# The low part of every fourth half tile of weights made by an accumulating DMA instead of by VectorE

## The chip, the core and the metric

The kernel runs on one core of a Trainium2 chip. The metric is device time in microseconds (us) for one execution; lower is better. A core has five engines with a queue each: TensorE (PE, matrix products; its weight loads are a row of their own, PEld), VectorE (DVE), ScalarE (ACT), GpSimd (POOL) and SyncE (SP, which here only issues DMAs). Engines work through their own queues in order and wait for each other by semaphores. Sixteen DMA engines move data; DMAs can be issued from SP's, ACT's and POOL's queues.

## What is computed

One layer of a decoder trunk on 256 tokens of width 2048, in float32:

```
h    = rmsnorm(x, pre_norm_g)
proj = h @ w_in                     # 2048 x 18448: keys, queries, values, gates of all heads
y_a  = (rmsnorm(gla_chunked(...)) * silu(a_g)) @ w_branch_a     # gated linear attention, 4 heads
y_b  = (rmsnorm(diff_attention(...)) * silu(b_g)) @ w_branch_b  # differential attention, 16 heads
merged = sigmoid(m_a) * y_a + sigmoid(m_b) * y_b
x    = x + rmsnorm(merged @ w_out, post_norm_g)
```

Nearly all the arithmetic is in the products with `w_in`, `w_branch_a`, `w_branch_b` and `w_out`, 2048 rows each, and each weight is used once.

## The kernel before

**Products in three parts.** TensorE multiplies in a rounded format (float32r). To keep float32's accuracy each operand is split into a high part (rounded) and a low part (the rest), and a product is hi x hi + hi x lo + lo x hi: three matmuls for one (`product`, L286). The activations are split once and stay in SBUF. The weights are split as they stream in.

**The weight stream** (L106 to L170). The host lays all weights out in the order of use. `chunk_plan` (L28) gives that order: values and low-rank gate, keys and queries of the linear attention, its output gates, two groups of differential heads, the 16 merge gates and branch-a products in turn, two more groups of heads, the merge gates of b, the branch-b products, the output projection. A tile of raw weights holds 2048 elements on each of 128 partitions (1 MB; less for the values) and is loaded by one DMA from SP's queue (L136) into one of three `raw` buffers. It is used in two halves of 1024. `emit_half` (L120) does one half: ScalarE copies it to float32r (`hi`, L155), and VectorE subtracts that from the raw half (`lo`, L156). The pool `wpool` has three buffers of each of `raw`, `hi` and `lo`. There are 392 halves; `take` (L163) hands out the next one and emits ahead as far as `AHEAD` = 4 halves. The last eight halves (`o3`) are kept for use twice and go to buffers of the pool `big`.

**The consumers.** `token_major` (L291) and `channel_major` (L306) take halves and issue 24 matmuls of 256 columns for a half, or 12 of up to 512. In a channel-major half the order of the three is (hi, xh), (hi, xl), (lo, xh).

**Head work between the products.** Forget gates, scores, softmax, head norms and transposes are written as generators in a list, `tasks`; `pump` (L280) lets them take a step behind each product or two, so their instructions stand between those of the stream on every engine. GpSimd does a few adds and the power -1/2 of the norms (`rsqrt`, L239). A scheduler then fixes each engine's order; the program's order of emission is what it goes by.

**Buffers.** `big` has 32 buffers of 4 KB a partition, one tag, for everything long-lived (split activations, gates, values, merged output). `small` holds short-lived tiles.

Of the kernel before, what the change touches and what calls it, by code (L numbers as in the profile page):

```python
# [6 lines left out]
F32 = mybir.dt.float32  # L7
F32R = mybir.dt.float32r
BF16 = mybir.dt.bfloat16
U8 = mybir.dt.uint8  # L10
AF = mybir.ActivationFunctionType
ALU = mybir.AluOpType
AX = mybir.AxisListType

P = 128
D = 2048
# [4 lines left out]
LEVELS = (1, 2, 4, 8, 16, 32, 64)  # L21
VG = (416, 416, 416, 416, 400)
RANK = 16
AHEAD = 4
WARM = 8


def chunk_plan():  # L28
    """Order of the weight chunks: (key, kind, source, columns, elements of a partition)."""
    plan = []  # L30
    at = 0
    for g, n in enumerate(VG):
        lr = RANK if g == 0 else 0
        plan.append((f"v{g}", "tok", "w_in", ([(6144, RANK)] if lr else []) + [(2048 + at, n - lr if lr else n)]))
        at += n - lr
    for hf in range(2):
        for name, base in (("k", 1024), ("q", 0)):
            for c in range(4):
                plan.append((f"{name}{hf}{c}", "chan", "w_in", [(base + 512 * hf + P * c, P)]))
    for g in range(4):  # L40
        plan.append((f"ag{g}", "tok", "w_in", [(4096 + 512 * g, 512)]))
    o = 6144 + RANK

    def heads(g):
        plan.append((f"dv{g}", "tok", "w_in", [(o + 4096 + 512 * g, 512)]))
        plan.append((f"bg{g}", "tok", "w_in", [(o + 6144 + 512 * g, 512)]))
        for pair in range(2):
            for n, name in enumerate(("dq", "dk")):
                for c in (2 * pair, 2 * pair + 1):
                    plan.append((f"{name}{g}{c}", "chan", "w_in", [(o + 2048 * n + 512 * g + P * c, P)]))  # L50

    def gate(br, f):
        plan.append((f"m{br}{f}", "chan", "w_in", [(o + 8192 + 2048 * br + P * f, P)]))

    def branch(br, f):
        plan.append((f"y{br}{f}", "chan", ("w_branch_a", "w_branch_b")[br], [(P * f, P)]))

    heads(0)
    heads(1)
    for f in range(KT):  # L60
        gate(0, f)
        branch(0, f)
    heads(2)
    heads(3)
    for f in range(KT):
        gate(1, f)
    for f in range(KT):
        branch(1, f)
    for g in range(4):
        plan.append((f"o{g}", "tok", "w_out", [(512 * g, 512)]))  # L70
    return plan
# [3 lines left out]
def hybrid_kernel(ctx: ExitStack, tc, xt, xn, preg, postg, w, w2, gkb, glag, lamv, diffg, ident_d, causal_d, lmask_d, out):  # L75
    nc = tc.nc
    pe, act, dve, pool, sp = nc.tensor, nc.scalar, nc.vector, nc.gpsimd, nc.sync

    const = ctx.enter_context(tc.tile_pool(name="const", bufs=1))
    wpool = ctx.enter_context(tc.tile_pool(name="wpool", bufs=3))  # L80
    big = ctx.enter_context(tc.tile_pool(name="big", bufs=32))
    small = ctx.enter_context(tc.tile_pool(name="small", bufs=2))
    psum = ctx.enter_context(tc.tile_pool(name="psum", bufs=4, space=bass.MemoryType.PSUM))

# [2 lines left out]
    def u(shape, name, dtype=F32):  # L87
        count[0] += 1
        return big.tile(shape, dtype, tag="u", name=f"{name}_{count[0]}")
# [13 lines left out]
    def f32(ap):  # L103
        return ap.bitcast(F32)

# [1 line left out]
    plan = chunk_plan()  # L107
    halves = []
    off = 0
    for key, kind, _, cols in plan:  # L110
        n = sum(c for _, c in cols)
# [5 lines left out]
    emitted = [0]  # L117
    raws = {}

    def emit_half():  # L120
        j = emitted[0]
        emitted[0] += 1
        key, at, size, h = halves[j]
        if h == 0:
            raws[at] = wpool.tile([P, 2048], F32, tag="raw", name=f"raw_{at}")
        raw = raws[at]
        src = w[at : at + P * size].rearrange("(p n) -> p n", p=P)
        n = size // 2
        fine = 2 if j == 0 else 1
        if h == 0:  # L130
            if j == 0:
                load_x(0, 1)
            elif j < 8:
                load_x(2 * j, 2)
            for a, b in ((0, n // 2), (n // 2, n), (n, size)) if j == 0 else ((0, n), (n, size)) if j < 8 else ((0, size),):
                i = sp.dma_start(raw[:, a:b], src[:, a:b])  # L136
                if j < 8:
                    tc.keep_in_program_order(i)
                if b == n // 2:
                    load_x(1, 1)  # L140
            if j < 8:
                load_x(2 * j + 2, 2)
        if j < 8:
            prep_x(2 * j)
            if j:
                prep_x(2 * j + 1)
        if key == "o3" and j + 1 < len(halves):
            hi_t, lo_t = u([P, 1024], "keep", F32R), u([P, 1024], "keep", F32R)
        else:
            hi_t = wpool.tile([P, 1024], F32R, tag="hi", name=f"hi_{j}")  # L150
            lo_t = wpool.tile([P, 1024], F32R, tag="lo", name=f"lo_{j}")
        for i in range(fine):
            a, b = n * i // fine, n * (i + 1) // fine
            r = raw[:, n * h + a : n * h + b]
            act.activation(hi_t[:, a:b], r, AF.Copy)  # L155
            dve.tensor_tensor(out=lo_t[:, a:b], in0=r, in1=f32(hi_t[:, a:b]), op=ALU.subtract)  # L156
            if j == 0 and i == 0:
                prep_x(1)
        ready[j] = (key, hi_t, lo_t)
# [3 lines left out]
    def take(key):  # L163
        j = used[0]
        used[0] += 1
        while emitted[0] < min(j + 1 + AHEAD, len(halves)):
            emit_half()
        name, hi, lo = ready.pop(j)
        assert name == key, (name, key)
        return hi, lo  # L170

# [1 line left out]
    xh = [u([P, 4, S], "xh", F32R) for _ in range(4)]  # L173
    xl = [u([P, 4, S], "xl", F32R) for _ in range(4)]
    preg_s = const.tile([P, KT], F32, name="preg_s")
# [4 lines left out]
    def load_x(kt, n):  # L180
        tc.keep_in_program_order(sp.dma_start(xraw[kt // 4][:, kt % 4 : kt % 4 + n, :], xt[:, kt : kt + n, :]))

    def prep_x(kt):
        i, j = kt // 4, kt % 4
        src = xraw[i][:, j, :]
        g = preg_s[:, kt : kt + 1]
        hi = xh[i][:, j, :]
        copied = act.activation(hi, src, AF.Copy, scale=g)  # L188
        if kt == 1:
            tc.keep_in_program_order(copied)  # L190
        dve.scalar_tensor_tensor(out=xl[i][:, j, :], in0=src, scalar=g, in1=f32(hi), op0=ALU.mult, op1=ALU.subtract)  # L191
# [76 lines left out]
        dve.tensor_scalar(out=neg_lam, in0=dots[:, 1:2], scalar1=dots[:, 0:1], scalar2=-LAM_INIT, op0=ALU.subtract, op1=ALU.add)  # L268
        dve.tensor_scalar(out=diffg_s, in0=diffg_s, scalar1=1.0 - LAM_INIT, scalar2=None, op0=ALU.mult)

# [1 line left out]
    def x_ops(kt):  # L272
        return xh[kt // 4][:, kt % 4, :], xl[kt // 4][:, kt % 4, :]

# [48 lines left out]
        act.activation(hi, bank, AF.Copy, scale=gain)  # L323
        dve.scalar_tensor_tensor(out=lo, in0=bank, scalar=gain, in1=f32(hi), op0=ALU.mult, op1=ALU.subtract)

# [1 line left out]
    vh = [u([P, 2, 512], "vh", F32R) for _ in range(4)]  # L327
    vl = [u([P, 2, 512], "vl", F32R) for _ in range(4)]
    lr = u([P, 2, P], "lr")
# [86 lines left out]
            lam()  # L416
            tasks.append(forget_gate())

# [1 line left out]
    att = [None, None]  # L420

    def view(t, off, *dims):
# [95 lines left out]
                pump(1)  # L518
        tasks.append(gla_scores(hf, ts["q"], ts["k"]))

# [1 line left out]
    oah = [u([P, 2, 2, S], "oah", F32R) for _ in range(4)]  # L522
    oal = [u([P, 2, 2, S], "oal", F32R) for _ in range(4)]

# [36 lines left out]
    gates = []  # L561
# [6 lines left out]
        if g % 2:  # L568
            tasks.append(gla_out(g // 2, gates[g - 1 :]))

# [1 line left out]
    obh, obl = [], []  # L572

    def diff_split(g, pair, tq, tk, q2, kh, kl):
# [103 lines left out]
            tasks.insert(0, diff_split(g, pair, *ts, *parts))  # L678
            tasks.append(diff_pair(g, pair, *parts, vv, uu))

# [1 line left out]
    def a_ops(kt):  # L682
        h, j = kt // 4, kt % 4
        i = 2 * (h // 2) + j // 2
        return oah[i][:, j % 2, h % 2, :], oal[i][:, j % 2, h % 2, :]
# [34 lines left out]
    for f in range(KT):  # L720
        o = channel_major(f"y1{f}", b_ops)
        i, j = f // 4, f % 4
# [4 lines left out]
        act.activation(hi, t, AF.Copy, scale=0.5)  # L727
        dve.scalar_tensor_tensor(out=ml[i][:, j, :], in0=t, scalar=0.5, in1=f32(hi), op0=ALU.mult, op1=ALU.subtract)

# [1 line left out]
    pg = [u([P, 1024], "pg") for _ in range(2)]  # L731
    for i in range(2):
        sp.dma_start(pg[i], postg[1024 * i : 1024 * i + 1024].partition_broadcast(P))
# [21 lines left out]
    def subtotal(b, parts):  # L755
        r = sm([P, 1], "or", bufs=2)
        dve.tensor_reduce(out=r, in_=ssq[:, b, :parts], op=ALU.add, axis=AX.X)
        dve.tensor_scalar(out=r, in0=r, scalar1=1.0 / D, scalar2=EPS, op0=ALU.mult, op1=ALU.add)
        return r
# [30 lines left out]
    for c in range(2):  # L790
        bank = ps("mm")
        for kt in range(KT):
            lo = 512 * (kt % 2) + 256 * c
# [3 lines left out]
        if c == 0:  # L797
            square(1, bank[:, :256], 256, 3)
            gain(1, bank[:, :256], 1536, 256)
            r = subtotal(1, 4)  # L800
# [61 lines left out]
```

## Time and profile before

| | us |
|---|---|
| median of two runs (1175.28 and 1175.64) | 1175.46 |
| profiled execution: span from first to last instruction | 1173.6 |
| TensorE matmul busy | 1160.6 |
| TensorE weight loads busy | 1088.4 |
| VectorE busy | 716.9 |
| of it the subtractions that make `lo`, 386 on L156 | 470.5 |
| ScalarE busy | 581.6 |
| of it the copies that make `hi`, 386 on L155 | 401.0 |
| GpSimd busy | 53.6 |

The profiled execution is one more execution than the two timed ones; the page gives its span, and no other time of it. The span is 1.86 us under the median of the timed runs. In the profile's rows a group reads: line, engine, operation, output<-inputs, sizes, count, then busy us and mean ns of one, then the idle time in front of it and what ended that. A row of the waits reads: who waited, on which line, for what; us in total, times, longest. A row of the table by stretches has the stretch and its length, then busy us and count of PE, PEld, DVE, ACT, POOL, then TensorE's granted clock, the DMA engines' busy share and GB/s. A row of DMA issues ends with the size of each and the median us from issue to landing. Matmuls are pipelined and their ends modelled, and a few matmul records can be missing.

### The profile page before, as it was taken

The numbers are of one execution on the slowest core, as the hardware profiler recorded it, in microseconds if no ns is written. First come the engines' busy times: TensorE is split into PE (matmuls) and PEld (weight loads), VectorE is DVE, ScalarE is ACT, GpSimd is POOL, SyncE is SP. The second block draws the span as 40 slices with busy tenths as digits, with TensorE's granted clock in tenths as the row PEclk, the third lists the DMA queues.
The fourth block names the chain that finished last, engine by engine and source line by source line (L and its number), as shares of the span: only waits on it lengthen the run. The fifth ranks groups of instructions, "written<-read, shape, count | busy, mean of one in ns | idle before, by whom it ended". The sixth has DMA issues, their size and how long they took to land.

```text
span 1173.6 us, 19130 instructions
## 1 busy us (share of the span) xinstructions
PE 1160.6 (99%) x7970; PEld 1088.4 (93%) x7970; DVE 716.9 (61%) x1054; ACT 581.6 (50%) x878; POOL 53.6 (5%) x53
## 2 busy tenths in 40 slices
PE   8999999999999999999999999999999999999997
PEld 6999999888889889999999998998999999999886
DVE  7556577657857766665554454565666655666454
ACT  7466343545645655545444334465555544444451
POOL 4010031001000000000000000000000000000000
PEclk9999999999999999999999999999999999999999
DMA  7755544545444444554455555544444445557561
GB/s 268 222 199 210 189 173 172 181 178 190 155 170 167 144 170 154 180 181 149 175 179 181 180 180 187 194 158 180 170 156 178 144 180 180 180 184 290 207 215 72
DMA packets 33799, 211.88 MB, mean 181 GB/s; under 512 B 4192, under 2 KB 5232, under 8 KB 11184
## 3 DMA queue, kind: packets, MB, share of 16 engines
q1 hardware_dynamic: 33104, 209.61, 50.8%
q8 instruction: 62, 1.02, 0.4%
q10 hardware_dynamic: 576, 1.05, 0.2%
q14 instruction: 25, 0.20, 0.1%
q0 software_dynamic: 32, 0.01, 0.0%
HBM read 208.55 MB, written 2.10 MB: 179 GB/s over the span
## 4 chain that ended last, share of the span: by engine, by line
PE 96%; issue 1%; ACT 1%; DVE 1%; DMA 0%; SPq 0%; DVEq 0%; POOLq 0%; POOL 0%; ACTq 0%
PE mm L288 91%; PE bg L484 1%; PE bg L601 1%; PE bg L604 1%; PE bg L288 1%; DMA xraw<-in_xt_dram 0%; PE bg L625 0%; PE bg L635 0%; PE bg L634 0%; PE bg L633 0%; PE bg L552 0%; PE bg L651 0%; ACT xh L188 0%; DVE xl L191 0%; DVE yg L773 0%
## 5 line engine op out<-in xcount | busy, mean ns | idle before, releaser
L156 DVE TENSOR_TENSOR lo<-raw,hi 128x1024 fp32r<-128x1024 f32 (+3 forms) x386 | 470.5, 1220 | 324.1 <-ACT hi L155 321.1
L155 ACT ACTIVATE hi<-raw 128x1024 fp32r<-128x1024 f32 (+3 forms) x386 | 401.0, 1040 | 496.9 <-PE mm L288 478.2
L288 PE MATMUL mm<-xh,hi 128*128 128x256 f32 x1280 | 365.4, 285 | 0.0
L288 PE MATMUL mm<-xh,lo 128*128 128x256 f32 x1280 | 362.2, 283 | 0.0
L288 PE MATMUL mm<-xl,hi 128*128 128x256 f32 x1280 | 362.1, 283 | 0.0
L288 PEld LDWEIGHTS mm<-xh,hi 128*128 128x128 f32 x1280 | 245.5, 192 | 1.5
L288 PEld LDWEIGHTS mm<-xl,hi 128*128 128x128 f32 x1280 | 245.5, 192 | 0.1
L288 PEld LDWEIGHTS mm<-xh,lo 128*128 128x128 f32 x1280 | 245.4, 192 | 0.0
L288 PE MATMUL mm<-hi,xh 128*128 128x512 f32 (+2 forms) x544 | 207.8, 383 | 1.2 <-ACT xh L188 0.9
L288 PE MATMUL mm<-lo,xh 128*128 128x512 f32 (+2 forms) x544 | 205.6, 378 | 2.4 <-DVE lo L156 2.4
L288 PE MATMUL mm<-hi,xl 128*128 128x512 f32 (+2 forms) x544 | 205.6, 378 | 0.8 <-DVE xl L191 0.7
L288 PEld LDWEIGHTS mm<-lo,xh 128*128 128x128 f32 x544 | 102.2, 188 | 18.4 <-DVE lo L156 3.7
L288 PEld LDWEIGHTS mm<-hi,xh 128*128 128x128 f32 x544 | 101.8, 188 | 17.7 <-ACT xh L188 1.3
L288 PEld LDWEIGHTS mm<-hi,xl 128*128 128x128 f32 x544 | 102.1, 188 | 17.1 <-DVE xl L191 1.7
L288 PE MATMUL mm<-oah,hi 128*128 128x256 f32 x256 | 72.8, 284 | 0.0
L288 PE MATMUL mm<-oah,lo 128*128 128x256 f32 x256 | 72.5, 283 | 0.0
L288 PE MATMUL mm<-obh,hi 128*128 128x256 f32 x256 | 72.4, 283 | 0.0
L288 PE MATMUL mm<-obl,hi 128*128 128x256 f32 x256 | 72.4, 283 | 0.0
L288 PE MATMUL mm<-obh,lo 128*128 128x256 f32 x256 | 72.4, 283 | 0.0
L288 PE MATMUL mm<-oal,hi 128*128 128x256 f32 x256 | 72.4, 283 | 0.0
L288 PEld LDWEIGHTS mm<-oah,hi 128*128 128x128 f32 x256 | 49.2, 192 | 0.0
L288 PEld LDWEIGHTS mm<-obh,hi 128*128 128x128 f32 x256 | 49.2, 192 | 0.0
(177 smaller groups left out, 1144.7 us busy)
## 6 DMA issues: line engine op xcount, KB each, us to landing
raw<-in_w_dram SPq DMA_DIRECT2D x176, 1024.0 KB, 4.8
raw<-in_w_dram SPq DMA_DIRECT2D x12, 832.0 KB, 5.6
raw<-in_w_dram SPq DMA_DIRECT2D x4, 800.0 KB, 4.4
raw<-in_w_dram SPq DMA_DIRECT2D x7, 416.0 KB, 6.9
xres<-in_xn_dram SPq DMA_DIRECT2D x4, 512.0 KB, 8.5
xraw<-in_xt_dram SPq DMA_DIRECT2D x7, 256.0 KB, 7.0
lmask<-in_lmask_dram SPq DMA_DIRECT2D x2, 512.0 KB, 8.1
pg<-in_postg_dram SPq DMA_DIRECT2D x2, 512.0 KB, 6.8
```

Source lines behind the costliest of these rows:

```text
L155: act.activation(hi_t[:, a:b], r, AF.Copy)
L156: dve.tensor_tensor(out=lo_t[:, a:b], in0=r, in1=f32(hi_t[:, a:b]), op=ALU.subtract)
L288: i = pe.matmul(out, lhs, rhs, start=first and n == 0, stop=last and n == len(pairs) - 1)
L484: pe.matmul(o, xk[:, P * c : P * c + P], xq.rearrange("p (b c t) -> p b c t", b=2, c=4)[:, :, c, :], start=i == 0, stop=i == 1)
L601: pe.matmul(banks[m][:, lo:up], q2[:, m, i2, t], kh[:, m, i2, :n], start=True, stop=False)
L604: pe.matmul(banks[m][:, lo:up], q2[r, m, i2, t], kl[r, i2, :n], start=False, stop=True)
```

## The change

For every fourth half from half 19 on (`queued`: j % 4 = 3, j at least 16, not in `o3`; 92 halves, always the second half of its raw tile) the low part is no longer made by VectorE. One emission earlier, ScalarE writes the negated, rounded half to a new tile `sum` (three buffers), and GpSimd issues a DMA that adds the raw half to it, SBUF to SBUF. The result, raw minus rounded, is used where `lo` was. `hi` is still made as before. Beside this, `raw` gets a fourth buffer, `AHEAD` becomes 5, `big` has 30 buffers in place of 32, and the scratch for the descriptors of DMAs issued by GpSimd is set to 4096. The other lines of the diff are comments.

```diff
-AHEAD = 4
+AHEAD = 5
...
-    big = ctx.enter_context(tc.tile_pool(name="big", bufs=32))
+    big = ctx.enter_context(tc.tile_pool(name="big", bufs=30))
...
+    sums = {}
+
+    def queued(j):
+        return j % 4 == 3 and 16 <= j < len(halves) and halves[j][0] != "o3"
+
     def emit_half():
...
-            raws[at] = wpool.tile([P, 2048], F32, tag="raw", name=f"raw_{at}")
+            raws[at] = wpool.tile([P, 2048], F32, tag="raw", name=f"raw_{at}", bufs=4)
...
         else:
+            if queued(j + 1):
+                sums[j + 1] = wpool.tile([P, 1024], F32R, tag="sum", name=f"sum_{j + 1}")
+                r = raw[:, n : 2 * n]
+                act.activation(sums[j + 1][:, :n], r, AF.Copy, scale=-1.0)
+                pool.dma_start(sums[j + 1][:, :n], r, accum_op=ALU.add)
             hi_t = wpool.tile([P, 1024], F32R, tag="hi", name=f"hi_{j}")
-            lo_t = wpool.tile([P, 1024], F32R, tag="lo", name=f"lo_{j}")
+            lo_t = sums.pop(j) if queued(j) else wpool.tile([P, 1024], F32R, tag="lo", name=f"lo_{j}")
...
             act.activation(hi_t[:, a:b], r, AF.Copy)
-            dve.tensor_tensor(out=lo_t[:, a:b], in0=r, in1=f32(hi_t[:, a:b]), op=ALU.subtract)
+            if not queued(j):
+                dve.tensor_tensor(out=lo_t[:, a:b], in0=r, in1=f32(hi_t[:, a:b]), op=ALU.subtract)
...
-    nc = bacc.Bacc("TRN2", target_bir_lowering=False, num_devices=1)
+    nc = bacc.Bacc("TRN2", target_bir_lowering=False, num_devices=1, dynamic_dma_scratch_size=4096)
```

## The prediction

> **What bounds the kernel now.** First the head of the page: how much of the span TensorE is busy, and at which clock. Then the two lists of what TensorE's matmul row and its weight-load row waited for, since only such waits can be won. Then a table by stretches, to see where in the span TensorE is idle.
>
> ```profile
> span 1173.6 us, 19130 instructions
> PE 1160.6 (99%) x7970; PEld 1088.4 (93%) x7970; DVE 716.9 (61%) x1054; ACT 581.6 (50%) x878; POOL 53.6 (5%) x53
> PEclk9999999999999999999999999999999999999999
> ...
> PE mm L288 <- DVE lo L156: 2.4, 2, 1.5
> ...
> PEld mm L288 <- DVE lo L156: 3.7, 4, 1.9
> ...
> 0.00:10.00 10.00, 7.87 (x33) 6.30 (x34) 4.11 (x9) 6.36 (x12) 2.17 (x8) 1.00 0.78 224
> ...
> 600.00:800.00 200.00, 200.00 (x1442) 189.35 (x1441) 108.37 (x141) 91.28 (x120) 1.75 (x2) 1.00 0.52 181
> ...
> 1150.00:1174.00 24.00, 15.96 (x116) 15.02 (x114) 7.38 (x15) 1.64 (x6) 1.10 (x2) 0.89 0.24 88
> ```
>
> TensorE is the bound: busy for 99% of the span, all 200 us of the middle stretch, at full clock (1.00). VectorE is at 61% and ScalarE at 50%. What TensorE ever waits for the low parts that VectorE makes is 2.4 us on the matmul row and 3.7 us on the weight-load row, six times in all. Were both lists taken away whole and added, that would be 6.1 us, 0.5% of the span. A measurement of this kernel can tell about 2% from no change; that is 23.5 us of the 1175.46. So relief for VectorE can't win that, and the question is only whether the new work makes TensorE wait.
>
> **How the pipeline breathes.** Three rows of ScalarE's timeline in the merge-gate and branch stretch, then the groups of the two instructions that split a half tile, and what the first waits for:
>
> ```profile
> 621.75 1.06 ACT L155 ACTIVATE hi<-raw 128x1024 fp32r<-128x1024 f32 x1 [1.57 <-PE mm L288]
> 624.62 1.06 ACT L155 ACTIVATE hi<-raw 128x1024 fp32r<-128x1024 f32 x1 [1.81 <-PE mm L288]
> ...
> 633.27 1.06 ACT L155 ACTIVATE hi<-raw 128x1024 fp32r<-128x1024 f32 x1 [1.58 <-PE mm L288]
> ...
> L156 DVE TENSOR_TENSOR lo<-raw,hi 128x1024 fp32r<-128x1024 f32 x345 | 427.4, 1239 | 298.3 <-ACT hi L155 295.6
> ...
> L155 ACT ACTIVATE hi<-raw 128x1024 fp32r<-128x1024 f32 x345 | 365.2, 1059 | 472.2 <-PE mm L288 456.6 <-issue 9.7 <-ACT prob L614 5.5
> ...
> ACT hi L155 <- PE mm L288: 478.2, 296, 2.7
> ```
>
> Four halves pass in 633.27 - 621.75 = 11.52 us, 2.88 us each. There are three buffers of hi, so the hi of half k starts when TensorE has done with half k-3: ScalarE waits 478.2 us in 296 waits for just that. So hi of half k starts two halves before TensorE starts half k, and TensorE has it in time by 2 x 2.88 - 1.06 = 4.7 us.
>
> **The change, part by part.** There are 392 halves; every fourth from half 19 to half 383 is done in the new way, 92 of them. I call such a half m.
>
> *VectorE loses 92 subtractions:* 92 x 1.239 = 114 us of its 716.9. Gain: nothing, since TensorE's six waits for lo are in the first 16 halves or so (the first stretch above has TensorE at 7.87 of 10 us, the middle none idle), and half 19 is the first that changes. I take 0; at most it is 6.1.
>
> *ScalarE gains 92 negations of the same shape as hi:* 92 x 1.059 = 97 us, 581.6 to 679, or 58%. That lies in its 472 us of waiting. What matters is where they stand in its queue. In the built order of the changed program 53 stand right ahead of the hi of half m-5, 33 ahead of that of m-6, four ahead of m-4, and two, for halves 27 and 31, one or two places ahead of their own. Each waits for its raw tile to land, and everything behind it on ScalarE waits too, the next hi first of all.
>
> So: when does raw land? The fourth raw buffer means that the tile with half m goes where the tile of half m-8 was, freed by ScalarE's hi of half m-8 (its VectorE reader is gone, its accumulating DMA was issued eight halves earlier). From the end of that hi to TensorE's start on m-6 there is the time from hi of m-8 to hi of m-4 (that hi starts as TensorE starts on m-6), less the hi itself: 11.52 - 1.06 = 10.46 us. In it must lie the load, the negation (1.06), hi (1.06) and, for the lo of m-6, 1.24 of VectorE, of which TensorE needs the result two matmuls later than hi, so about 1.0; some 0.2 for hand-overs. That leaves 7.1 us for the load from issue to landing where the negation stands ahead of m-6, and 7.1 + 2.88 = 10.0 ahead of m-5.
>
> ```profile
> q1 hardware_dynamic: 33104, 209.61, 50.8%
> ...
> raw<-in_w_dram SPq DMA_DIRECT2D x176, 1024.0 KB, 4.8
> ...
> DMA to landing us min/median/max: 2.6/4.8/8.9
> ...
> xres<-in_xn_dram SPq DMA_DIRECT2D x4, 512.0 KB, 8.5
> ...
> preg_s<-in_preg_dram POOLq DMA_DIRECT2D x1, 8.0 KB, 2.7
> ...
> 1.23 0.71 POOL L176 DMA_DIRECT2D preg_s<-in_preg_dram  x1 [0.79 <-POOLq L855]
> ```
>
> The median load takes 4.8 us, within both. In the new kernel it shares the 16 DMA engines with an accumulating transfer, which is issued at about the same point (behind the negation of half m-4). Queue q1 moved 209.61 MB in 50.8% of 1173.6 us: 596 us, or 2.98 us for a tile of 1.049 MB and 1.49 for half a tile. No accumulating DMA is in the trace, so its engine time is bounded: below by 1.49 (it moves as much as a plain copy), above by the nearest slow row, the 512 KB of xres at 8.5 us to landing, the whole of it charged to the engines. I take twice a plain copy, 2.98, nearer to the lower end: the transfer reads two half tiles (raw and the negated one) for each that it writes, and the q1 row, the only one of engine time alone, is that end. The DMA share then goes from 0.508 by 92 x 2.98 / 1173.6 = 0.234 to 0.74: not the bound. A load's landing becomes 4.8 us (no overlap) to 4.8 + 2.98 = 7.8 (full overlap). Spread evenly, 23% are over 7.1, by 0.34 us on average: 0.08 us for each of the 33 sites, 2.6 us; nothing at the 53 sites with 10.0.
>
> [...]
>
> *POOL gains 92 DMA issues.* Its one issue in the trace took 0.71 us for 128 rows: 92 x 0.71 = 65 us on an engine that is 5% busy. An issue waits for the negation, and the rsqrt instructions of the heads queue behind it, as the issues queue behind them. Is the transfer itself late? Where the negation stands ahead of m-5 and raw lands as late as it may, TensorE's start on m is still 5 x 2.88 + 1.06 + 1.0 = 16.5 us off when the negation is done; issue and transfer at the slow bound need 0.71 + 8.5 = 9.2. Hidden by 7 us; by 4 at the four sites ahead of m-4. Only halves 27 and 31 are near: one microsecond for both.
>
> *Delays on ScalarE and POOL that reach TensorE through head work:* a negation that waits for raw holds exponentials and evacuations back by as much as the load is late. That head work is issued one or two halves ahead; its PE instructions follow a pump of 2 x 2.88 us. I take 2 us in all, between 0 and 16 heads x 1 us.
>
> *SP:* the loads of the tiles of m wait for the DMA of m-8 as well, issued some 20 us before; 0. *AHEAD 5, 30 big buffers, the smaller descriptor scratch:* AHEAD changes the program's order alone, since three hi buffers still hold hi back; the two big buffers cost at most what shows now for reuse of them,
>
> ```profile
> SPq L733 <- PE mm L288: 0.2, 1, 0.2
> ...
> SPq L739 <- PE mm L288: 0.2, 1, 0.2
> ```
>
> so 0; the scratch holds the descriptors of one transfer at a time when they come each 11.5 us; 0.
>
> **Sum.** 2.6 + 1 + 2 = 5.6 us on the span: 1179.2. The median of the runs, 1175.46, stands 1.86 above the span of 1173.6, so 1181.0.
>
> **Rivals.** *Slower: the accumulating transfer is slow enough to hold the loads.* If it costs four plain copies (6.0 us), the engines' share is 0.508 + 92 x 5.96 / 1173.6 = 0.98, and a load in full overlap lands after 10.8 us. Evenly spread from 4.8 to 10.8, 62% are over 7.1 by 1.85 us on average (33 x 1.14 = 38 us), 13% over 10.0 by 0.4 (53 x 0.05 = 3 us): 1173.6 + 41 + 3 + 1.86 = 1219. At three copies (4.47) the same working gives 33 x 0.53 = 18 and 1196. So it decides at little over three; at six, the share is over 1.2 and the DMA engines would be the bound, 1400 and more. For it: nothing in the trace says that an add is cheap, the limit of 7.1 is close to the 4.8, and the longest load was already 8.9. Against it: the two reads are the only extra work that the change names. *Nothing shows:* load and transfer seldom overlap, since the engines are half idle; then 1175.5 plus or minus 2. *Faster:* VectorE's 114 us shorten the head work and the waits above; at most 6.1, so 1169.4; it would need TensorE's matmuls themselves to run faster to be over 2%, and they run at clock 1.00 with nothing idle between.
>
> **The numbers.** Forecast (1177 to 1199, by twofold cost) 0.43; nothing shows (1173 to 1177) 0.22; slow transfer (over 1199, from three and a half copies up) 0.33; faster 0.02, all of it short of 2% or nearly. The predicted time is 1181. The range goes from 1172, which leaves out only the last case, to 1235, which takes in about half of the slow case (four copies and a little); what is left out is about 0.18. Faster by over 2%: 0.01; within: 0.66; slower: 0.33.
>
> **What would show it.** Right: PE still 99% busy; L156 with about 92 fewer; a group of 92 negations on ScalarE at 1.06 us, with 100 us or so of waits for raw's DMA in front; DMA share about 0.74; few PE waits for hi or lo, all of them a microsecond or less. Wrong: a software queue that takes far more than 23% of the engines; loads with a median over 7 us; PE waiting for ScalarE's hi or VectorE's lo each fourth half; PE waiting for the accumulating DMA itself, which would mean that a transfer takes over 16 us.

## The result and the profile after

| | before | after |
|---|---|---|
| median of two runs, us | 1175.46 (1175.28, 1175.64) | 1190.05 (1186.49, 1193.61) |
| ratio to before, 95% interval | | 1.0122 [1.0091, 1.0153] |
| profiled execution: span, us | 1173.6 | 1184.6 |

The changed kernel is 1.2% slower. That lies inside the forecast range, but 9 us over the 1181 that was forecast. The profiled execution, which is the run of 1186.49, had a mean granted clock of 0.999. The run of 1193.61 us had a span of 1191.7 at 0.993, and 0.006 x 1190 = 7.1 us is the difference between the two spans; the clocks are rounded to a thousandth, which is 1.2 us, and that run left no trace. So two things are to be explained: 11.0 us in the profiled span, and a lower clock in the other run.

The page of the changed kernel, in the order of the lines shown of before (head, groups, queues, issues):

```profile
span 1184.6 us, 19478 instructions
PE 1164.4 (98%) x7970; PEld 1087.7 (92%) x7970; DVE 603.6 (51%) x962; ACT 664.7 (56%) x970; POOL 131.8 (11%) x145
PEclk9999999999999999999999999999999999999999
...
q1 hardware_dynamic: 33104, 209.61, 49.2%
q0 software_dynamic: 13280, 47.63, 21.8%
...
L165 ACT ACTIVATE hi<-raw 128x1024 fp32r<-128x1024 f32 (+3 forms) x386 | 398.2, 1036 | 295.9 <-PE mm L299 282.0
L167 DVE TENSOR_TENSOR lo<-raw,hi 128x1024 fp32r<-128x1024 f32 (+3 forms) x294 | 357.2, 1217 | 323.4 <-ACT hi L165 321.4
...
L158 ACT ACTIVATE sum<-raw 128x1024 fp32r<-128x1024 f32 (+2 forms) x92 | 96.4, 1048 | 161.9 <-DMA raw<-in_w_dram 161.9
L159 POOL DMA_DIRECT2D sum<-raw x92 | 79.6, 865 | 871.5 <-ACT sum L158 683.1
...
raw<-in_w_dram SPq DMA_DIRECT2D x176, 1024.0 KB, 5.9
sum<-raw POOLq DMA_DIRECT2D x86, 512.0 KB, 5.7
...
xres<-in_xn_dram SPq DMA_DIRECT2D x4, 512.0 KB, 12.7
```

VectorE is 716.9 - 603.6 = 113 us lighter, ScalarE 83 us heavier, and TensorE still has the same 7970 matmuls. The new queue q0 took 21.8% of 16 engines' span: 0.218 x 1184.6 / 92 = 2.81 us for one accumulating transfer. Queue q1 took 0.492 x 1184.6 = 583 us for 209.61 MB, which is 1.46 us for half a tile. The transfer costs 1.9 plain copies.

The waits of ScalarE, then those of TensorE's matmul row and of its weight-load row:

```profile
ACT hi L165 <- PE mm L299: 282.0, 211, 2.6
ACT sum L158 <- DMA raw<-in_w_dram: 161.9, 83, 5.3
```

```profile
PE mm L299 <- DVE lo L167: 5.3, 6, 1.6
PE bg L662 <- DVE ogb L657: 1.6, 2, 1.2
PE mm L299 <- ACT hi L165: 1.5, 3, 0.7
PE bg L370 <- DVE lrt L357: 1.4, 1, 1.4
...
PE mm L299 <- DMA sum<-raw: 0.2, 1, 0.2
```

```profile
PEld mm L299 <- DVE lo L167: 9.3, 11, 1.9
```

ScalarE's waiting has changed hands: of the 478 us that it waited for TensorE to free a buffer of `hi`, 196 are gone, and 162 stand in front of the negations, in 83 of 92 cases, for a raw tile that has not landed. TensorE itself hardly ever waits for the accumulating DMA (0.2 us on the matmul row, 0.6 on the weight-load row). It waits for `lo` and `hi` that are late, and for head work (`ogb`, `lrt`).

By stretches (stretch, length, busy us of PE, PEld, DVE, ACT, POOL, clock, DMA share, GB/s), first the changed kernel:

```profile
200.00:350.00 150.00, 148.51 (x709) 123.93 (x708) 84.50 (x104) 85.69 (x105) 21.87 (x21) 1.00 0.70 211
350.00:600.00 250.00, 250.00 (x1878) 238.00 (x1877) 133.61 (x270) 150.88 (x254) 23.04 (x28) 1.00 0.70 207
600.00:800.00 200.00, 200.00 (x1465) 190.39 (x1465) 86.92 (x119) 105.76 (x130) 16.35 (x19) 1.00 0.74 226
800.00:960.00 160.00, 158.37 (x1156) 148.52 (x1155) 82.12 (x189) 96.96 (x179) 16.17 (x19) 1.00 0.66 202
...
1070.00:1150.00 80.00, 78.39 (x409) 66.87 (x408) 37.93 (x41) 42.46 (x51) 5.14 (x6) 1.00 0.85 276
```

and two of the same stretches before:

```profile
200.00:350.00 150.00, 150.00 (x731) 126.68 (x731) 101.47 (x117) 76.52 (x94) 9.81 (x8) 1.00 0.49 173
...
1070.00:1150.00 80.00, 80.00 (x387) 67.62 (x387) 46.35 (x47) 38.46 (x47) 0.00 (x0) 1.00 0.59 213
```

Nothing is lost from 350 to 800 us, where TensorE is busy all the time although the DMA share went from about 0.5 to 0.7. Before, TensorE is busy all of 200 to 350, 800 to 960 and 1070 to 1150 us as well. The loss sits in the values and the linear attention (up to 350), in the late heads (800 to 960) and in the output projection (1070 to 1150).

One case in full, from the chain of work in the values (start, us, what):

```profile
103.57 6.73 DMA raw<-in_w_dram
...
110.39 0.04 ACT sum L158
...
111.35 1.05 ACT hi L165
...
112.42 1.24 DVE lo L167
...
113.70 4.33 PE mm L299 x34
```

Read it downwards. A tile lands 6.7 us after its issue. The negation of its second half (half 47) has been at the head of ScalarE's queue for 2.95 us, and only then runs. Behind it stands the `hi` of half 42, five halves earlier in the stream, whose own data has long been there. Then VectorE makes the `lo`, and TensorE, which had been without work for 0.95 us, goes on. The late load belongs to a half that TensorE needs only five halves later; it is the order on ScalarE that makes it late for half 42.

The same through head work, ScalarE's timeline in the third group of heads:

```profile
816.17 1.06 ACT L158 ACTIVATE sum<-raw 128x1024 fp32r<-128x1024 f32 x1 [5.20 <-DMA raw<-in_w_dram]
817.14 0.39 ACT L625 ACTIVATE prob<-prob,mx 128x128 f32<-128x128 f32 x1
```

VectorE had the `mx` that this exponential reads at 813.17; the exponential began at 817.14, behind a negation that waited 5.20 us. The head norm that follows comes late, and TensorE's transposes of `ogb` wait for 1.4 us at 824.

### The profile page after: what moved, and what is told of

It reads as the page before. It is cut to its first block, busy times and chain, and to the rows that moved or that the text cites. A ratio compares the mean times of both kernels' runs of the same rounds, so it can differ in the third digit from the quotient of the medians.

```text
span 1184.6 us, 19478 instructions
## 1 busy us (share of the span) xinstructions
PE 1164.4 (98%) x7970; PEld 1087.7 (92%) x7970; DVE 603.6 (51%) x962; ACT 664.7 (56%) x970; POOL 131.8 (11%) x145
## 3 DMA queue, kind: packets, MB, share of 16 engines
q1 hardware_dynamic: 33104, 209.61, 49.2%
q0 software_dynamic: 13280, 47.63, 21.8%
q10 hardware_dynamic: 576, 1.05, 0.2%
## 4 chain that ended last, share of the span: by engine, by line
PE 87%; DMA 5%; ACT 2%; issue 2%; DVE 2%; POOL 1%; SPq 0%; DVEq 0%; POOLq 0%; ACTq 0%
PE mm L299 82%; DMA raw<-in_w_dram 5%; ACT hi L165 1%; PE bg L495 1%; DVE lo L167 1%; PE bg L612 1%; PE bg L615 1%; PE bg L299 1%; DMA sum<-raw 1%; PE bg L636 0%; ACT xh L199 0%; ACT sum L158 0%; PE bg L662 0%; PE bg L563 0%; PE bg L646 0%
## 5 line engine op out<-in xcount | busy, mean ns | idle before, releaser
L167 DVE TENSOR_TENSOR lo<-raw,hi 128x1024 fp32r<-128x1024 f32 (+3 forms) x294 | 357.2, 1217 | 323.4 <-ACT hi L165 321.4
L299 PE MATMUL mm<-xh,lo 128*128 128x256 f32 x1024 | 289.9, 283 | 0.7 <-DVE lo L167 0.7
L299 PEld LDWEIGHTS mm<-xh,lo 128*128 128x128 f32 x1024 | 196.2, 192 | 1.0 <-DVE lo L167 0.9
L158 ACT ACTIVATE sum<-raw 128x1024 fp32r<-128x1024 f32 (+2 forms) x92 | 96.4, 1048 | 161.9 <-DMA raw<-in_w_dram 161.9
L159 POOL DMA_DIRECT2D sum<-raw x92 | 79.6, 865 | 871.5 <-ACT sum L158 683.1
L299 PE MATMUL mm<-lo,xh 128*128 128x512 f32 (+2 forms) x424 | 160.5, 379 | 4.0 <-DVE lo L167 3.8
L299 PEld LDWEIGHTS mm<-lo,xh 128*128 128x128 f32 x424 | 79.6, 188 | 18.0 <-DVE lo L167 7.2
L299 PE MATMUL mm<-xh,sum 128*128 128x256 f32 x256 | 72.5, 283 | 0.0
L299 PE MATMUL mm<-obh,lo 128*128 128x256 f32 x192 | 54.3, 283 | 0.0
## 6 DMA issues: line engine op xcount, KB each, us to landing
xres<-in_xn_dram SPq DMA_DIRECT2D x4, 512.0 KB, 12.7
```

Of the source, the lines that this page charges most:

```text
L158: act.activation(sums[j + 1][:, :n], r, AF.Copy, scale=-1.0)
L159: pool.dma_start(sums[j + 1][:, :n], r, accum_op=ALU.add)
L299: i = pe.matmul(out, lhs, rhs, start=first and n == 0, stop=last and n == len(pairs) - 1)
```

## Experiments

All times are medians in us, with the range and the number of runs; a ratio is to the kernel before, run beside it on the same chip (1175.72 beside experiments 1 to 4, 1175.93 beside the others), with its 95% interval.

**1. The side edits alone.** No half is queued; the fourth `raw` buffer, `AHEAD` 5, 30 buffers and the scratch stay.

```diff
-        return j % 4 == 3 and 16 <= j < len(halves) and halves[j][0] != "o3"
+        return False and 16 <= j < len(halves) and halves[j][0] != "o3"
```

> The changed kernel without its core: AHEAD 5, four raw buffers, 30 big buffers and the small scratch stay, but no half is made in the new way, VectorE makes all low parts. Theory (the negation's wait for raw holds ScalarE, and all that TensorE loses comes from that): no loss, 1175 +- 2 us. Rival A (the side edits cost part of it, two buffers fewer or another order): 1178 or more.

Measured: 1176.45 (1175.97 to 1176.89, 11), ratio 1.0005 [0.9996, 1.0014]. The side edits cost nothing.

**2. The negation pinned to its place in the program,** right ahead of the `hi` of half m-1, where the source has it.

```diff
-                act.activation(sums[j + 1][:, :n], r, AF.Copy, scale=-1.0)
+                tc.keep_in_program_order(act.activation(sums[j + 1][:, :n], r, AF.Copy, scale=-1.0))
```

> The changed kernel with each negation pinned in ScalarE's queue behind everything emitted before it, so right ahead of the hi of half m-1 instead of m-5 or m-6; negations, transfers and bytes stay the same. Theory (ScalarE is held by a negation whose raw half has not landed): ScalarE's 162 us of waiting for raw fall under 20 us, TensorE's waits for lo and for head work go; the transfer now has about 4 x 2.88 - 2.1 = 9.4 us for 0.85 of issue and a median of 5.7, so a few TensorE waits for sum may come instead; 1174 to 1180. Rival B (the sharing of the DMA engines itself costs the time): as the changed kernel, 1186 to 1190.

Measured: 1213.62 (1210.29 to 1216.83, 4), ratio 1.0321 [1.0303, 1.0338]. My number was missed by far. ScalarE's wait for raw is gone, as expected, but TensorE now waits for the transfer, by its weight-load row:

```profile
PEld mm L299 <- DMA sum<-raw: 34.0, 37, 3.4
```

```profile
sum<-raw POOLq DMA_DIRECT2D x86, 512.0 KB, 9.5
```

In this trace the negation begins as the `hi` of half m-2 ends, and its own end lies a median of 9.9 us ahead of TensorE's turn to half m (halves 79 to 359). So the time was there that I had reckoned with (9.4 us). It was the transfer that took longer, a median of 9.5 us from issue to landing against 5.7 in the changed kernel. So this run does not separate the theories: it takes the first wait away and puts a worse one in its place. Experiments 6 to 8 were made to stand between the two.

**3. The early negation without the DMA.** VectorE adds the raw half to the negated one, at the place where it made `lo`.

```diff
-                pool.dma_start(sums[j + 1][:, :n], r, accum_op=ALU.add)
...
-            if not queued(j):
+            if queued(j):
+                dve.tensor_tensor(out=lo_t[:, a:b], in0=r, in1=f32(lo_t[:, a:b]), op=ALU.add)
+            else:
```

> The changed kernel with the negations where they are, but VectorE adds raw to the negated half, and no accumulating DMA is issued. Theory: without the second transfer loads land after a median of 4.8 us again, under the 7.1 and 10.0 us that they have; ScalarE still waits for raw in front of some negations, but TensorE does not feel it; 1175 to 1179. Rival C (a negation that far ahead holds ScalarE too long whatever the DMA engines do): 1183 or more. Rival B: 1175.

Measured: 1176.09 (1175.82 to 1176.75, 11), ratio 1.0003 [0.9995, 1.0012].

```profile
ACT sum L158 <- DMA raw<-in_w_dram: 59.4, 37, 3.4
```

The negations stand ahead here too and still wait for raw, but 59 us in 37 waits instead of 162 in 83, none longer than 3.4. The pipeline has that much slack. The 92 negations on ScalarE cost nothing, and their early place alone costs nothing.

**4. The transfers without the early negation.** The 92 accumulating DMAs go onto three idle tiles, which nobody reads; VectorE makes every `lo`.

```diff
+    idle = [const.tile([P, 1024], F32R, name=f"idle_{i}") for i in range(3)]
...
-                act.activation(sums[j + 1][:, :n], r, AF.Copy, scale=-1.0)
-                pool.dma_start(sums[j + 1][:, :n], r, accum_op=ALU.add)
+                pool.dma_start(idle[(j + 1) // 4 % 3][:, :n], r, accum_op=ALU.add)
...
```

> All low parts made by VectorE, no negation; GpSimd still issues the 92 accumulating DMAs, of the same size, onto three tiles that nothing reads. This adds the load on the DMA engines alone. Theory: loads land later (a median of about 5.9 us, DMA share about 0.7) but only hi waits for them, with half a dozen halves of room; 1175 to 1178. Rival B (sharing of the DMA engines, or GpSimd's issues beside VectorE, cost the time): 1184 to 1190.

Measured: 1180.12 (1179.78 to 1180.61, 5), ratio 1.0037 [1.0024, 1.0049].

```profile
600.00:800.00 200.00, 200.00 (x1459) 190.14 (x1458) 107.52 (x136) 89.20 (x115) 16.34 (x19) 1.00 0.77 229
```

```profile
PE mm L299 <- ACT hi L166: 5.5, 1, 5.5
```

The DMA share is as high as in the changed kernel and a load's median is the same 5.9 us, and TensorE does not idle in the middle. The 4.6 us by which this span exceeds that of before is one wait of 5.5 us, up to 10.3 us, long before the first of these transfers (42.9 us): the order at the start came out otherwise. At TensorE's turn to half 15 (46 us in before) it is 4.1 us behind before, at the end 4.6. So the busier DMA engines cost at most half a microsecond. Taken with experiment 3: neither half of the change costs anything to speak of by itself. It is the two together.

**5. The changed kernel again,** on this chip.

> The changed kernel itself once more, beside the others of this call. Both theories: 1186 to 1194; ScalarE waits some 160 us for raw in front of negations.

Measured: 1188.46 (1186.17 to 1189.94, 4), ratio 1.0105 [1.0090, 1.0120].

**6 to 8. The negation at a chosen place.** The loads are emitted earlier, and the negation is fixed ahead of the `hi` of m-3, m-2 or m-4. Here the m-3 form; the other two have another number and chain the instructions of ScalarE one behind the other.

```diff
-            if queued(j + 1):
...
+            if queued(j + 3):
+                m = j + 3
...
+                        sp.dma_start(raws[at_c][:, :size_c], w[at_c : at_c + P * size_c].rearrange("(p n) -> p n", p=P))
...
+                tc.keep_in_program_order(act.activation(sums[m][:, :nm], r, AF.Copy, scale=-1.0))
+                pool.dma_start(sums[m][:, :nm], r, accum_op=ALU.add)
```

> The changed kernel with every negation fixed right ahead of the hi of half m-3 (the load of its tile is emitted in time for that). Negations, transfers and bytes as in the changed kernel. Theory (only the place in ScalarE's queue decides: too early and it waits for raw, too late and TensorE waits for the transfer): the load has 7.1 + 3 x 2.88 = 15.7 us, over the longest landing seen (13.7), and the transfer with its issue has 5 x 2.88 - 1.06 - 1.06 = 12.3, over the 10.4 that the median took when pinned late and about the longest; TensorE loses nearly nothing, 1175 to 1178. Rival B (two streams on the DMA engines cost time wherever the negation stands): 1184 or more.

> The same with the negation right ahead of the hi of half m-2. Theory: the transfer with its issue has 4 x 2.88 + 0.75 - 2.1 + 2.88 - 2.88 = about 10 to 12 us, near its median; TensorE waits a little for sum: 1178 to 1195, between the one ahead of m-3 and the pinned one (1213.6). Rival B: as the changed kernel, 1186 to 1190.

> The same with the negation right ahead of the hi of half m-4. Theory: the load has 7.1 + 2 x 2.88 = 12.9 us, a little under the longest landing (13.7), and the transfer 15 us, over all seen: 1175 to 1178. Rival B: 1184 or more.

| place of the negation | median (range, runs) | ratio | transfer's landing, 512 KB | ScalarE's wait for raw ahead of it |
|---|---|---|---|---|
| m-1 (experiment 2) | 1213.62 (1210.29 to 1216.83, 4) | 1.0321 [1.0303, 1.0338] | 9.5 | none |
| m-2 | 1177.12 (1176.53 to 1178.03, 10) | 1.0010 [1.0001, 1.0020] | 4.7 | none |
| m-3 | 1176.54 (1176.07 to 1176.77, 10) | 1.0005 [0.9995, 1.0014] | 6.4 | 2.0 in 2 |
| m-4 | 1177.01 (1176.74 to 1177.71, 10) | 1.0010 [1.0001, 1.0019] | 5.2 | 5.6 in 5 |
| m-5 and m-6, by the scheduler (experiment 5) | 1188.46 (1186.17 to 1189.94, 4) | 1.0105 [1.0090, 1.0120] | 5.6 | 158.9 in 79 |

The same 92 transfers, the same negations, the same work on every engine: what differs is the place on ScalarE, and between m-2 and m-4 the loss is gone. The loads are emitted earlier too, but they do not start earlier: at the 92 tiles a load is issued a median of 0.03 us behind the `hi` that frees its buffer, in the changed kernel and in all three of these. Nor is it that the loads got shorter: at m-4 those of the 92 tiles take a median of 6.2 us, as in the changed kernel, and ScalarE waits 5.6 us for them in place of 161.9. This is the test that settles the cause.

At m-2 I had allowed for some loss, on the 9.5 us landing of the pinned form; it landed in 4.7. The traces show what differs. Between 200 and 1060 us, of a transfer's median of 9.4 us ahead of m-1, a load of raw was in flight too for 7.0; ahead of m-2, for 2.4 of 4.6. So the transfers that had loads beside them for longer also took longer; that the loads are the cause is not shown, since no run changes the meeting alone. None of the three is faster than the kernel before: the best, 1176.54, has an interval that takes in 1.

**9. A plain copy in place of the add,** at the scheduler's places. The kernel leaves the add out, so the low part of these halves holds the raw half.

```diff
-                pool.dma_start(sums[j + 1][:, :n], r, accum_op=ALU.add)
+                pool.dma_start(sums[j + 1][:, :n], r)
```

> The changed kernel with a plain copy in place of the accumulating transfer, same tiles, same place, same queue (so the add is left out and the low part of these 92 halves holds the raw half). Theory (an accumulating transfer costs the DMA engines two copies): the software queue's share falls from 21.8% to about 11%, loads land after some 5.3 us, ScalarE waits under 130 us for raw, and 1177 to 1183. Rival D (any second stream does it, the add costs nothing): the share stays at 20% or more and 1186 or more.

Measured: 1180.14 (1177.10 to 1186.16, 10), ratio 1.0042 [1.0025, 1.0059].

```profile
q0 software_dynamic: 13280, 47.63, 11.2%
```

```profile
ACT sum L158 <- DMA raw<-in_w_dram: 123.0, 70, 5.1
```

The engine time of q0 falls from 21.8% to 11.2%: the add doubles what the transfer costs the engines. A load's median falls from 5.9 to 5.4, ScalarE's wait from 162 to 123 us, and less than half of the loss is left (0.42% against 1.05%). So the engine time of the transfer does matter, through the loads that it lengthens for an order that waits for them. By how much, this run tells only roughly: it scatters over 9 us, and in its profile 2.9 of the 7.0 us of TensorE's gaps between 40 and 1160 us lie behind one `lo` of VectorE that took 6.5 us (see the hardware section).

**10. Twice as many transfers, ahead of m-3:** every second half, 184 in all, with ScalarE's instructions chained as in experiments 7 and 8.

```diff
-        return j % 4 == 3 and 16 <= j < len(halves) and halves[j][0] != "o3"
+        return j % 2 == 1 and 16 <= j < len(halves) and halves[j][0] != "o3"
```

> The negation fixed ahead of the hi of half m-3, as in the run at 1176.5, but for every second half from half 17 on, 184 in all. DMA share 0.51 + 2 x 0.21 = 0.93. Theory (place decides while the engines have room): transfers and loads land later than 6.5 and 5.4 us, but in 12.3 and 15.7 most still do; 1177 to 1200. Rival B (the DMA engines become the bound): over 1200, with TensorE waiting for sum every second half.

Measured: 1189.43 (1188.25 to 1193.25, 4), ratio 1.0125 [1.0107, 1.0143].

```profile
120.00:170.00 50.00, 48.08 (x388) 47.88 (x388) 21.83 (x21) 25.49 (x26) 14.07 (x14) 0.97 1.01 278
...
600.00:800.00 200.00, 200.00 (x1472) 190.81 (x1471) 65.31 (x98) 123.41 (x155) 31.14 (x36) 1.00 0.96 270
```

At a DMA share of 0.96 TensorE is busy for all 200.00 us of this stretch of the gates when the place is right. From 120 to 170 us, where the share reaches 1.01 (it adds up the packets' times, so it can pass 1), TensorE idles for 1.9 us, but not for a transfer: that gap lies behind one `lo` that took 5.8 us on VectorE (see the hardware section). In all, the profile has 9.2 us of gaps on the weight-load row between 40 and 1160 us and three falls of the clock (0.96 over the first 40 us, 0.83 from 160 to 170 and from 1100 to 1110 us). So the loss of this kernel does not show that the DMA engines are its bound, and where they would become one stays open; no run here changes their load alone at that share.

**11. Half as many, at the scheduler's places:** every eighth half, 46 in all.

```diff
-        return j % 4 == 3 and 16 <= j < len(halves) and halves[j][0] != "o3"
+        return j % 8 == 7 and 16 <= j < len(halves) and halves[j][0] != "o3"
```

> The changed kernel, with its scheduler's places (five or six halves ahead), for every eighth half, 46 in all (two fall elsewhere at the start). Theory: each early negation can hold ScalarE, so about half of the loss stays: 1179 to 1184. Rival (the loss is a matter of the overall DMA share, which is 0.62 here): within 2 us of before.

Measured: 1177.30 (1175.87 to 1177.98, 10), ratio 1.0010 [1.0001, 1.0020]. I expected about half of the loss; a tenth of it is left. That is what the rival had named, by which the loss is a matter of the DMA share alone; what speaks against the rival is experiments 6 to 8, which lose nothing at the full share.

```profile
ACT sum L158 <- DMA raw<-in_w_dram: 32.8, 19, 4.7
```

With half the transfers, ScalarE waits a fifth as long. The loss is not proportional to the number of sites. With fewer transfers the loads land sooner too (a median of 5.0 us), and there is slack, as experiment 3 showed: the waits cost only where they exceed it.

## Why the prediction was right and wrong

**TensorE as the bound, no gain from VectorE: right.** The 113 us came off VectorE (114 predicted) and bought nothing. A change of 2% was not the least that can be told here, as the prediction had it: the experiments' intervals are 0.2 to 0.4% wide. The kernel with the negation ahead of m-3, which has VectorE's relief without the stalls, is not faster than before.

**92 negations hidden: right.** They took 96.4 us (97 predicted), and experiment 3 runs them at no cost. (GpSimd's 92 issues took 79.6 us, 65 predicted.) In the trace the negations stand where the prediction had them: 53 ahead of m-5, 33 ahead of m-6, four ahead of m-4, the two for halves 27 and 31 ahead of m-1 and m-2.

**The transfer as two plain copies: right.** 2.81 us against 2.98 predicted, a DMA share of 0.49 + 0.22 = 0.71 against 0.74, a load's median of 5.9 us against the assumed spread from 4.8 to 7.8. The rival of a slow transfer, from three and a half copies up, fell with it. A plain copy in the same place shows the same ratio: 11.2% of the engines' span in experiment 9 against 21.8%. That the price comes from two reads for each write was the author's estimate; no run shows the reads, and q0 has the same 13280 packets and 47.63 MB with the add and without.

**The mechanism: right.** A negation hoisted five or six halves ahead waits in ScalarE's in-order queue (161.9 us in 83 waits) for a load that the transfer has lengthened (a median of 5.9 us against 4.8 before), and holds what stands behind it. Experiments 3, 4 and 6 to 8 show it. One sign of being right failed: TensorE's waits for `hi` and `lo` were to be a microsecond or less, and behind 40 us three on its weight-load row were longer, up to 1.35.

**The sum of 5.6 us: wrong, it was 11.0 in the profiled span.** TensorE's weight-load row has 13 gaps of over 0.25 us between 40 and 1160 us, 11.7 us in all, where before has one of 0.39 that is in both. The terms, side by side:

| step of the prediction | predicted | measured |
|---|---|---|
| `hi` and `lo` late, 33 sites ahead of m-6 | 2.6 | 0.6 |
| the same, 53 sites ahead of m-5 (and four ahead of m-4) | 0 | 3.6 |
| transfer late for halves 27 and 31 | 1 | 0.6 |
| head work late | 2 | 3.8 |
| output projection, loads behind others | 0 | 2.8 |
| sum (of the unrounded terms) | 5.6 | 11.3 |

The terms were off both ways, two downward and three upward. That the time still fell inside the forecast's 1177 to 1199 is owed to the width of that range; the sum itself gave half of the loss.

The step that failed is "nothing at the 53 sites with 10.0". I worked out the time that a load has from halves of 2.88 us and from a ScalarE queue that holds only `hi` copies. Both hold in the merge gates, where nothing was lost, and fail elsewhere. In the values halves pass faster, as three rows of ScalarE's timeline of before show, whose copies wait for TensorE to get through such halves:

```profile
100.12 1.06 ACT L155 ACTIVATE hi<-raw 128x1024 fp32r<-128x1024 f32 x1 [0.18 <-PE mm L288]
102.35 1.06 ACT L155 ACTIVATE hi<-raw 128x1024 fp32r<-128x1024 f32 x1 [1.17 <-PE mm L288]
104.46 1.06 ACT L155 ACTIVATE hi<-raw 128x1024 fp32r<-128x1024 f32 x1
```

In the case shown above three of the five halves pass at 2.2 us and two, of the keys, at 2.88, so the limit of 10.0 becomes 10.0 - 3 x 0.7 = 7.9. The rest went on ScalarE, which is busy without a break from 95.6 to 107.4 us there, mostly with head work, and which has the negation of half 43 ahead of the `hi` of half 39, from whose end the load's time counts:

```profile
100.74 1.10 ACT L158 ACTIVATE sum<-raw 128x1024 fp32r<-128x1024 f32 x1
...
102.64 0.90 ACT L165 ACTIVATE hi<-raw 128x800 fp32r<-128x800 f32 x1
```

That `hi` ended at 103.55, and TensorE turned to half 42 at 112.45, 8.9 us later. Negation, `hi`, `lo` and hand-overs at the prediction's own prices (1.06 + 1.06 + 1.0 + 0.2 = 3.3; the hand-overs in the chain above are 0.09, 0.02 and 0.04) leave 5.6 us for a load that took 6.73: 1.1 late, for a gap of 0.95.

In the linear attention the pace is about as I took it, but head work stands between. The case at 256 us has these pieces in its chain:

```profile
241.83 8.66 DMA raw<-in_w_dram
...
253.30 3.02 DVE lo L167
...
256.37 1.66 PE mm L299 x6
```

A load of 8.66 us is followed by the negation, a `tanh`, two instructions of VectorE's head work and a `lo`, and TensorE has a gap of 1.35. The `lo` took 3.1 us in place of 1.24 while GpSimd worked on its own part of the linear attention; with one of 1.24 the gap would not be there, by an estimate from these rows and all else equal. So this 1.35 of the 3.6 us needed both, the late load and the slow `lo`, and the prediction had no term for the second.

At the sites ahead of m-6, where I had looked for the loss, the spread of landings was not the even one that I assumed. There the negation began a median of 5.6 us behind the end of the `hi` of m-8, and later than 7.1 in four of 33 cases, where the even spread gave eight. Two of the three gaps in head work, at 824 and 927 us, came from these sites as well (2.1 us).

**SP at 0: wrong at one place.** Toward the end the loads of the output projection's tiles meet the loads for the post-norm and the residual, issued from the same queue. The chain there:

```profile
1079.00 13.73 DMA raw<-in_w_dram
...
1094.84 7.10 DMA raw<-in_w_dram
```

One load takes 13.7 us to land. It was issued 2.4 to 4.1 us behind the four loads of the residual, which were still under way, as was an accumulating transfer, issued at 1076.09, that took 11.8. The longest load of before was 8.9, at the same place and with the same loads of the residual; xres itself went from 8.5 to 12.7 us. I had looked at SP for waits only, not for a stretch where the DMA engines already carry other loads. The side edits at 0 were right (ratio 1.0005 in experiment 1); what the descriptor scratch holds at a time was an estimate, and no run shows it.

**The term that was absent: the clock.** The profiled execution kept its clock, and its run time is 1186.49, 5.5 over the forecast. The median is higher by the second run, whose mean clock was 0.993. The last section has gaps with a clock of 0.50 behind them, in other profiles; what lowered the clock in that run is not known. In the repetition of experiment 5 the profiled span was 1188.1 at 0.996, with gaps of 12.5 us in all, about as many as here.

**What stays open.** How much of the loss, in the runs that left no trace, is owed to a slow `lo` on VectorE; and the last microsecond of the m-2, m-4 and every-eighth kernels, whose intervals just exclude 1.

## What to carry to other kernels

When work is handed to a DMA, look at where the scheduler puts the instruction that feeds it: here ScalarE, which works in order, waited 161.9 us for loads ahead of the negations and held everything behind it, and a lead of five or six half tiles over the consumer, as here (ratio 1.0105), can be worse than one of two to four (1.0005 to 1.0010). Choose the place so that both times fit, the load ahead of the instruction and the transfer behind it, and work the limits out for the fastest stretch of the kernel and for its busiest engines, not for the steady one. Relieving an engine that the bound hardly waits for bought nothing here, even with the new work as well hidden as at m-3 (ratio 1.0005).

## What the runs showed of the hardware

**TensorE's granted clock was 0.50 for about 3.4 us behind some of its gaps, and stayed at 1.00 behind others.** From the kernel of experiment 10, by stretches (the clock is the third column from the end), after a gap of 2.1 us on its weight-load row that ended at 162.45:

```profile
162.00:163.00 1.00, 0.55 (x4) 0.55 (x5) 1.00 (x3) 0.34 (x1) 1.00 (x2) 1.00 0.65 127
163.00:164.00 1.00, 1.00 (x10) 1.00 (x9) 1.00 (x1) 0.00 (x0) 0.94 (x2) 0.97 1.18 184
164.00:165.00 1.00, 1.00 (x7) 1.00 (x6) 1.00 (x2) 0.00 (x0) 0.90 (x1) 0.50 0.94 123
...
167.00:168.00 1.00, 1.00 (x9) 1.00 (x9) 0.01 (x1) 0.96 (x2) 0.00 (x0) 0.83 0.97 328
```

By these rows the clock falls to 0.50 at 163.94, 1.5 us after TensorE has work again, and comes back about 3.4 us later, so by an estimate from them this one event costs 1.7 us beside the gap. In the pinned form (experiment 2) TensorE's matmul row was busy for 0.46 of the 3 us up to 1102; the clock was 0.67 from 1103 to 1104, 0.50 up to 1106, 0.62 in the next us and 1.00 from 1107 on.

It does not follow every gap. In the profile of experiment 5 a gap of 2.7 us at 164 us left the clock at 1.00, while two gaps of 1.5 and 1.1 at 1105.6 and 1106.9 were followed by 0.50. In the profiled execution of the changed kernel no gap up to 1150 us was, neither the longest, 1.71 us up to 83.4 on the weight-load row, nor the two of 1.16 and 1.07 there, close together, up to 1105.3. What decides whether the clock falls, no run here shows. The kernels with gaps scatter by several microseconds (1186.17 to 1189.94 in experiment 5) and those of experiments 6 to 8 by 0.7 to 1.5; how much of that is the clock's is not shown either: the four spans of experiment 5, 1184.3, 1185.9, 1187.3 and 1188.1, had clocks of 0.997, 0.999, 0.998 and 0.996.

**Some of VectorE's subtractions took up to 6.9 us in place of 1.24, beside work of GpSimd.** The 345 `lo` of 1024 elements in the kernel before have a mean of 1.24 us. In the profile of experiment 5 one took this long:

```profile
156.96 6.87 DVE L167 TENSOR_TENSOR lo<-raw,hi 128x1024 fp32r<-128x1024 f32 x1 [0.39 <-ACT hi L165]
```

Meanwhile GpSimd ran five operations of the linear attention, one behind the other, from 156.84 to 163.74 us. In the profiles of the kernel before and of the changed one 564 such `lo` (337 and 227) have no work of GpSimd beside them (DMA issues aside), and none of them took over 1.27 us; the seven that took longer, 1.4 to 3.1 us, all have. Five of them are in the kernel before (the longest 3.1 us, at 154 us), and there TensorE felt none of it. With the negation ahead of m-3 one of 4.7 us passed without a gap, but one of 6.9 us cost TensorE 2.7 us in experiment 5, one of 6.5 cost 2.9 in experiment 9, and one of 5.8 cost 2.1 in experiment 10. Not every operation of GpSimd goes with a slow `lo`: in those two profiles 33 of the 40 `lo` beside its work took 1.23 us or less. No experiment here changes GpSimd's work, so that it is the cause is not shown.

**An accumulating DMA within SBUF cost twice a plain one in engine time, but far less than twice in landing.** It took 21.8% of the engines' span in the changed kernel and a plain copy in its place 11.2%. Its median landing was 5.7 us against 5.9 for a load of twice the size from memory, and the plain copy landed in 4.8.
